# Moving one 256-token scale broadcast from behind a stage's last transposes to between its last two groups of transposes

## The chip, the cores and the metric

The kernel runs on one core of a Trainium2 chip. The metric is the device time of one execution in microseconds (us). PE is the matrix engine (TensorE; PEld is its weight loads), DVE the vector engine, ACT the scalar engine, POOL is GpSimd, SP issues most transfers.

## What is computed

One transformer-like block on 256 tokens of width 2048, then a final RMSNorm, all in float32. Cut to what the change touches:

```python
def rms_norm(x, w):
    y = xf * lax.rsqrt(jnp.mean(xf * xf, axis=-1, keepdims=True) + NORM_EPS)
    return y * w

def reference(...):
    n = rms_norm(h, norm_mix_w)
    h = h + token_mixer(n, ...)          # 8 delta heads, 8 x 3 windowed heads, then w_out
    n = rms_norm(h, norm_ffn_w)          # the second norm
    h = h + conv_gated_mlp(n, w_ffn_in, conv_ffn_w, w_ffn_out)   # 2048 -> 2 x 5632 -> 2048
    return rms_norm(h, norm_final_w)
```

The second norm has two factors: the weight `norm_ffn_w` by channel and the reciprocal root by token. The kernel applies the first when it transposes `h`, and the second, which commutes with the matrix product, only to the results of `w_ffn_in`.

## The kernel before, in words

**Weights.** All weight matrices stream through four raw buffers (`raws`, 1 MB each) by transfers that SP issues (`refill`, line 255). The products have float32 accuracy made of fast passes: each piece of weights is split into a high part `hi` (ACT, line 265) and a rest `lo` (DVE, line 266), each in four buffers, and activations are held as high and low halves too (`xcat[:, k, :256]` and `xcat[:, k, 256:]` for the 16 blocks k of 128 channels).

**Items.** The work of PE is a list of items. An item of `cm_block` (lines 303 to 322) covers one half of the 2048 input channels for 128 output channels: eight blocks k, three matmuls each (lines 314, 315, 316: `hi` with the high half of `xcat`, `hi` with its low half, `lo` with its high half), so 24 matmuls of 128x128 weights on 256 columns, into one PSUM bank. An item of `v_slab` (lines 382 to 384) has the tokens as weights, also 24 matmuls of 256 columns. Items of `tm_group` (lines 1224 to 1226, for `w_out` and `w_ffn_out`) use 512 columns. `run_items` splits the weights of three items ahead, writes one item's matmuls, then calls `pump`, which lets side work put its instructions behind that item. So the order on every engine is fixed when the program is written; nothing is scheduled later.

**Side work** consists of generators: each step up to a `yield` is one packet of instructions. `g_norm2(s, hb)` is one, for each quarter s of the 2048 channels of `h`: it squares and sums `h` by token (ACT, line 1275), then for each of two pairs of channel blocks takes a spare PSUM bank from `SB` (two banks), transposes four 128x128 tiles on PE (line 1282), writes the high half of `xcat` with the channel weight (ACT, line 1286) and the low half (DVE, line 1290). For s = 3, the last quarter, it then finishes the scale by token: sum and mean on DVE (lines 1295, 1296), the power -1/2 on POOL (line 1297), and two matmuls with the identity that spread the 256 scales over 128 partitions (line 1301), copied to `rbc` by ACT (line 1302). `rbc` (it lies in the tile `rC`) is first read by `up_hook` (line 1378), when the first output block of `w_ffn_in` is complete.

**The join of the two stages.** The stage of `w_ffn_in` has 22 x 8 = 176 items. Its first eight are reordered: first the four that read the channel blocks 0 to 7, then the four that read 8 to 15, so that matmuls can start before the last quarter of `h` is transposed. Five items of the stage run (`run_items(n_out + 5)`) while the side work of the second norm is still being written; `flush` then writes what is left of it. The 171 items that follow have no side work on PE at all.

Of the kernel before, what the change touches and what calls it, by code (L numbers as in the profile page):

```python
# [7 lines left out]
AF = mybir.ActivationFunctionType  # L8
ALU = mybir.AluOpType

P = 128
T = 256
D = 2048
# [5 lines left out]
EPS = 1e-6  # L19
# [66 lines left out]
def block_kernel(tc, A, out, dbg=None):  # L86
# [4 lines left out]
    ACT = nc.scalar.activation  # L91
    V = nc.vector
    G = nc.gpsimd
    mm = nc.tensor.matmul
# [15 lines left out]
    def pool(name, **kw):  # L110
        g = tc.tile_pool(name=name, bufs=1, reuse_waits="tile", **kw)
        return g, g.__enter__()
# [11 lines left out]
    SB = Slots(banks[6:8])  # L124

    cst = cp.tile([P, C_N], F32, name="cst")
    ident = cst[:, C_ID : C_ID + P]
    tri = [cst[:, C_TRI + o * P : C_TRI + (o + 1) * P] for o in range(2)]
    blk = cst[:, C_BLK : C_BLK + P]
    neghalf = cp.tile([P, 8], F32, name="neghalf")  # L130
# [10 lines left out]
    ss = cp.tile([P, 8, 2, H], F32, name="ss")  # L141
# [18 lines left out]
    done = set()  # L160
# [66 lines left out]
    def take(slots):  # L227
        while not slots.free:
            yield 0
        return slots.get()  # L230
# [221 lines left out]
    for k2 in range(8):  # L452
        bk = DB.get()
# [755 lines left out]
    go, op = None, None  # L1209
# [41 lines left out]
    go, op = pool("outp", side="left")  # L1251
# [3 lines left out]
    hss = cp.tile([P, 2, 4], F32, name="hss")  # L1255
    rbc = rC
# [5 lines left out]
    def o_hook(s):  # L1262
        hb = hs[s % 2]
        for t in range(2):
            V.tensor_add(hb[:, t, :], obanks[s][t], xr[s % 2][:, t, :])
        if s < 2:
            nc.gpsimd.dma_start(xr[s], xtok[:, :, (s + 2) * 512 : (s + 3) * 512])
        nc.gpsimd.dma_start(h_tok[:, :, s * 512 : (s + 1) * 512], hb)
        spawn(g_norm2(s, hb))
# [3 lines left out]
    def g_norm2(s, hb):  # L1273
        for t in range(2):
            ACT(sq, hb[:, t, :], AF.Square, accum_out=hss[:, t, s : s + 1])
        yield 0
        for k2 in range(2):
            bk = yield from take(SB)
            for e in range(2):
                kl = 2 * k2 + e  # L1280
                for t in range(2):
                    nc.tensor.transpose(bk[:, e * T + t * P : e * T + (t + 1) * P], hb[:, t, kl * P : (kl + 1) * P], ident)
            for e in range(2):
                k = 4 * s + 2 * k2 + e
                src = bk[:, e * T : (e + 1) * T]
                ACT(xcat[:, k, :T], src, AF.Copy, scale=nw_ffn[:, k : k + 1])
            for e in range(2):
                k = 4 * s + 2 * k2 + e
                src = bk[:, e * T : (e + 1) * T]
                stt(xcat[:, k, T:], src, nw_ffn[:, k : k + 1], xcat[:, k, :T].bitcast(F32), op0=ALU.mult, op1=ALU.subtract)  # L1290
            SB.put(bk)
            yield 700
        done.add(("n2", s))
        if s == 3:
            V.tensor_reduce(out=ss[:, 0, 0:2, 0:1], in_=hss, axis=mybir.AxisListType.X, op=ALU.add)
            V.tensor_scalar(ss[:, 1, 0:2, 0:1], ss[:, 0, 0:2, 0:1], 1.0 / D, EPS, op0=ALU.mult, op1=ALU.add)
            G.tensor_tensor(ss[:, 2, 0:2, 0], ss[:, 1, 0:2, 0], neghalf[:, 0:2], op=ALU.pow)
            yield 300
            bk = yield from take(SB)
            for t in range(2):  # L1300
                mm(bk[:, t * P : (t + 1) * P], lhsT=ss[:, 2, t, 0:1].to_broadcast([P, P]), rhs=ident, start=True, stop=True)
            ACT(rbc, bk[:, :T], AF.Copy)
            SB.put(bk)
            done.add("rbc")
            yield 0

# [179 lines left out]
```

## Time and profile before

| | us |
|---|---|
| three runs | 1543.66, 1540.58, 1543.41; median 1543.41 |
| the profiled execution | 1541.09, its span 1539.3 |
| PE busy in the span | 1513.6 (98%), 11531 matmuls |
| DVE, ACT, POOL busy | 1039.7 (68%), 828.2 (54%), 168.7 (11%) |
| PE busy from 792 to 1291 (the stage of `w_ffn_in`) | 499.00 of 499.00, granted clock 1.00 |
| PE busy from 1291 to 1539 (`w_ffn_out` and the end) | 239.75 of 248.00 |

A matmul's record lasts longer than the time to the next one's start, because matmuls overlap; the time from start to start is what PE spends on each. The granted clock is a share of 2.4 GHz. One matmul with float32 operands, as in line 1301, leaves two records in the trace, so the broadcast's two matmuls show as four; a transpose leaves one.

### The profile page before, as it was taken

What the parts mean: (1) busy time and instruction counts of PE and PEld (TensorE: products, weight loads), DVE (VectorE), ACT (ScalarE), POOL (GpSimd) and SP (SyncE); (2) the same over time, 40 slices, a digit from 0 to 9 for tenths busy, and PEclk for the clock granted to TensorE, in tenths of its full rate; (3) what the DMA queues carried; (4) which work ended last, traced back from release to release, by engine and by line L of the source; (5) the groups of instructions that cost most, each with busy time, mean ns of one, the idle gap of its engine ahead of it and who ended that gap; (6) DMA issues with size and microseconds to landing.
All of it is one profiled execution on the core that took longest, in us unless ns stands there. A gap on an engine that the chain in (4) does not pass through costs nothing.

```text
span 1539.3 us, 28194 instructions
## 1 busy us (share of the span) xinstructions
PE 1513.6 (98%) x11531; PEld 1442.5 (94%) x11531; DVE 1039.7 (68%) x1703; ACT 828.2 (54%) x1430; POOL 168.7 (11%) x257
## 2 busy tenths in 40 slices
PE   7999999999999999998999999999999999999997
PEld 7999999999999999997889999999999999888886
DVE  5878978879865666764557777677776766455454
ACT  5598875645556546653555545454454454344342
POOL 3254553000022202100000000000000000000000
PEclk9999999999999999998999999999999999999999
DMA  9657789746667636633765565565655557566552
GB/s 255 220 182 225 235 293 231 223 152 193 191 155 238 218 115 194 211 133 133 259 210 192 166 206 177 187 197 166 206 176 188 195 167 265 197 206 205 192 191 82
DMA packets 247699, 301.21 MB, mean 196 GB/s; under 512 B 11397, under 2 KB 208182, under 8 KB 247186
## 3 DMA queue, kind: packets, MB, share of 16 engines
q1 hardware_dynamic: 235602, 269.81, 54.8%
q0 software_dynamic: 11536, 29.02, 6.1%
q8 instruction: 90, 1.47, 0.4%
q10 hardware_dynamic: 432, 0.59, 0.1%
q14 instruction: 39, 0.32, 0.1%
HBM read 285.69 MB, written 13.65 MB: 194 GB/s over the span
## 4 chain that ended last, share of the span: by engine, by line
PE 95%; ACT 2%; issue 1%; DVE 1%; DMA 0%; POOL 0%; POOLq 0%; SPq 0%; ACTq 0%; DVEq 0%
PE bank L314 20%; PE bank L316 20%; PE bank L315 20%; PE bank L1224 7%; PE bank L1225 7%; PE bank L1226 7%; PE bank L382 3%; PE bank L383 3%; PE bank L384 3%; PE bank L978 1%; PE bank L1024 1%; PE bank L1019 1%; ACT hi L265 1%; PE bank L1198 1%; DMA xt<-in_x_dram 0%
## 5 line engine op out<-in xcount | busy, mean ns | idle before, releaser
L266 DVE TENSOR_TENSOR lo<-raw,hi 128x1024 fp32r<-128x1024 f32 x504 | 620.9, 1233 | 394.8 <-ACT hi L265 392.4
L265 ACT ACTIVATE hi<-raw 128x1024 fp32r<-128x1024 f32 x504 | 533.6, 1060 | 554.9 <-PE bank L315 252.1
L314 PE MATMUL bank<-xcat,hi 128*128 128x256 f32 x2688 | 757.5, 282 | 0.3 <-ACT pad L329 0.3
L315 PE MATMUL bank<-xcat,hi 128*128 128x256 f32 x2688 | 751.2, 279 | 0.0
L316 PE MATMUL bank<-xcat,lo 128*128 128x256 f32 x2688 | 751.0, 279 | 0.0
L315 PEld LDWEIGHTS bank<-xcat,hi 128*128 128x128 f32 x2688 | 511.2, 190 | 0.0
L314 PEld LDWEIGHTS bank<-xcat,hi 128*128 128x128 f32 x2688 | 505.7, 188 | 2.9 <-issue 0.9
L316 PEld LDWEIGHTS bank<-xcat,lo 128*128 128x128 f32 x2688 | 504.8, 188 | 0.0
L1225 PE MATMUL bank<-lo,gth 128*128 128x512 f32 x336 | 130.8, 389 | 0.0
L1226 PE MATMUL bank<-hi,gtl 128*128 128x512 f32 x336 | 130.8, 389 | 0.0
L1224 PE MATMUL bank<-hi,gth 128*128 128x512 f32 x336 | 130.8, 389 | 0.0
L382 PE MATMUL bank<-hi,xcat 128*128 128x256 f32 x384 | 109.2, 284 | 0.0
L384 PE MATMUL bank<-hi,xcat 128*128 128x256 f32 x384 | 107.0, 279 | 0.0
L383 PE MATMUL bank<-lo,xcat 128*128 128x256 f32 x384 | 107.0, 279 | 0.0
L1226 PEld LDWEIGHTS bank<-hi,gtl 128*128 128x128 f32 x336 | 63.1, 188 | 13.1
L1224 PEld LDWEIGHTS bank<-hi,gth 128*128 128x128 f32 x336 | 63.1, 188 | 13.1
L1225 PEld LDWEIGHTS bank<-lo,gth 128*128 128x128 f32 x336 | 63.1, 188 | 12.9
L382 PEld LDWEIGHTS bank<-hi,xcat 128*128 128x128 f32 x384 | 72.6, 189 | 0.5
L384 PEld LDWEIGHTS bank<-hi,xcat 128*128 128x128 f32 x384 | 72.4, 189 | 0.0
L383 PEld LDWEIGHTS bank<-lo,xcat 128*128 128x128 f32 x384 | 72.2, 188 | 0.0
L1391 DVE SCALAR_TENSOR_TENSOR fy<-fpad,cwf,fy 128x256 f32<-128x256 f32 x132 | 63.5, 481 | 2.4
L1421 POOL DMA_DIRECT2D nfb<-in_norm_final_w_dram x1 | 0.6, 585 | 485.7 <-PE bank L316 485.7
(299 smaller groups left out, 1447.9 us busy)
## 6 DMA issues: line engine op xcount, KB each, us to landing
raw<-in_w_in_dram SPq DMA_DIRECT2D x104, 1024.0 KB, 5.5
raw<-in_w_ffn_in_dram SPq DMA_DIRECT2D x88, 1024.0 KB, 5.1
raw<-in_w_ffn_out_dram SPq DMA_DIRECT2D x44, 1024.0 KB, 5.0
raw<-in_w_out_dram SPq DMA_DIRECT2D x14, 1024.0 KB, 5.1
rec_d<-rec POOLq DMA_DIRECT2D x8, 768.0 KB, 7.4
rr<-rec_d POOLq DMA_DIRECT2D x6, 512.0 KB, 4.6
xt<-in_x_dram SPq DMA_DIRECT2D x4, 512.0 KB, 8.4
gam<-cg_d POOLq DMA_DIRECT2D x8, 256.0 KB, 7.5
```

The lines of the kernel that those rows point to most:

```text
L265: ACT(hi, src, AF.Copy)
L266: V.tensor_sub(lo, src, hi.bitcast(F32))
L314: mm(acc, lhsT=hi[:, kk, :], rhs=xcat[:, k, :T], start=k == 0, stop=False)
L315: mm(acc, lhsT=hi[:, kk, :], rhs=xcat[:, k, T:], start=False, stop=False)
L316: mm(acc, lhsT=lo[:, kk, :], rhs=xcat[:, k, :T], start=False, stop=k == KT - 1)
L382: mm(o, lhsT=xh, rhs=hi[:, kk, :], start=k == 0 and t == 0, stop=False, skip_group_check=True)
L383: mm(o, lhsT=xh, rhs=lo[:, kk, :], start=False, stop=False, skip_group_check=True)
L384: mm(o, lhsT=xl, rhs=hi[:, kk, :], start=False, stop=k == KT - 1, skip_group_check=True)
L1224: mm(a[t], lhsT=xh, rhs=hi[:, kk, :], start=st, stop=False)
L1225: mm(a[t], lhsT=xh, rhs=lo[:, kk, :], start=False, stop=False)
L1226: mm(a[t], lhsT=xl, rhs=hi[:, kk, :], start=False, stop=sp_)
L1391: stt(y, pad[:, d : d + T], cwf[:, d, b : b + 1], y, op0=ALU.mult, op1=ALU.add)
```

## The change

For the last quarter (s = 3) the sum, mean and power move ahead of the first `yield`, in front of both groups of transposes, and the two broadcast matmuls with their copy move in front of the second group (`k2` = 1). Nothing is added or dropped.

```diff
     def g_norm2(s, hb):
         for t in range(2):
             ACT(sq, hb[:, t, :], AF.Square, accum_out=hss[:, t, s : s + 1])
+        if s == 3:
+            V.tensor_reduce(out=ss[:, 0, 0:2, 0:1], in_=hss, axis=mybir.AxisListType.X, op=ALU.add)
+            V.tensor_scalar(ss[:, 1, 0:2, 0:1], ss[:, 0, 0:2, 0:1], 1.0 / D, EPS, op0=ALU.mult, op1=ALU.add)
+            G.tensor_tensor(ss[:, 2, 0:2, 0], ss[:, 1, 0:2, 0], neghalf[:, 0:2], op=ALU.pow)
         yield 0
         for k2 in range(2):
+            if s == 3 and k2:
+
+                bk = yield from take(SB)
+                for t in range(2):
+                    mm(bk[:, t * P : (t + 1) * P], lhsT=ss[:, 2, t, 0:1].to_broadcast([P, P]), rhs=ident, start=True, stop=True)
+                ACT(rbc, bk[:, :T], AF.Copy)
+                SB.put(bk)
+                done.add("rbc")
+                yield 0
             bk = yield from take(SB)
...
         done.add(("n2", s))
-        if s == 3:
-            V.tensor_reduce(out=ss[:, 0, 0:2, 0:1], in_=hss, axis=mybir.AxisListType.X, op=ALU.add)
-            V.tensor_scalar(ss[:, 1, 0:2, 0:1], ss[:, 0, 0:2, 0:1], 1.0 / D, EPS, op0=ALU.mult, op1=ALU.add)
-            G.tensor_tensor(ss[:, 2, 0:2, 0], ss[:, 1, 0:2, 0], neghalf[:, 0:2], op=ALU.pow)
-            yield 300
-            bk = yield from take(SB)
-            for t in range(2):
-                mm(bk[:, t * P : (t + 1) * P], lhsT=ss[:, 2, t, 0:1].to_broadcast([P, P]), rhs=ident, start=True, stop=True)
-            ACT(rbc, bk[:, :T], AF.Copy)
-            SB.put(bk)
-            done.add("rbc")
-            yield 0
```

How the order of instructions moves. The changed file has its own line numbers: there the broadcast is line 1286, its copy 1287, the transposes 1295, the high halves 1299, the low halves 1303, the sum and mean 1277 and 1278. Each "..." below stands for the rest of an item's 24 matmuls.

PE at the join of the stages, before (`hs` holds `h`, `cst` the identity, `ss` the scales; the items' banks are 71 to 74):

```order
L1282 MATMUL bank_77<-cst,hs_8008 128x128 x4
L314 MATMUL bank_71<-xcat,hi_100 128x256
...
L1282 MATMUL bank_78<-cst,hs_8008 128x128 x4
L314 MATMUL bank_72<-xcat,hi_101 128x256
...
L314 MATMUL bank_73<-xcat,hi_98 128x256
...
L1301 MATMUL bank_77<-cst,ss 128x128 x2
L314 MATMUL bank_74<-xcat,hi_99 128x256
```

The broadcast is the last thing that stands between items; behind it come 171 items in one row.

PE at the same place, with the change:

```order
L1295 MATMUL bank_77<-cst,hs_8008 128x128 x4
L314 MATMUL bank_71<-xcat,hi_100 128x256
...
L1286 MATMUL bank_78<-cst,ss 128x128 x2
L314 MATMUL bank_72<-xcat,hi_101 128x256
...
L1295 MATMUL bank_77<-cst,hs_8008 128x128 x4
L314 MATMUL bank_73<-xcat,hi_98 128x256
...
L314 MATMUL bank_74<-xcat,hi_99 128x256
```

There are still three groups between the same items, one item apart now, but the last one consists of four transposes and stands directly in front of the first item that reads the channel blocks 8 to 15. From that item on 172 items follow in one row.

ACT at the same place, before:

```order
L1286 ACTIVATE xcat<-bank_77,nw_ffn 128x256 x2
L265 ACTIVATE hi_99<-raw_94 128x1024
L1286 ACTIVATE xcat<-bank_78,nw_ffn 128x256 x2
L265 ACTIVATE hi_100<-raw_95 128x1024
L265 ACTIVATE hi_101<-raw_95 128x1024
L1302 ACTIVATE rC<-bank_77 128x256
```

and with the change:

```order
L1299 ACTIVATE xcat<-bank_77,nw_ffn 128x256 x2
L265 ACTIVATE hi_99<-raw_94 128x1024
L1287 ACTIVATE rC<-bank_78 128x256
L265 ACTIVATE hi_100<-raw_95 128x1024
L1299 ACTIVATE xcat<-bank_77,nw_ffn 128x256 x2
L265 ACTIVATE hi_101<-raw_95 128x1024
```

The copy to `rC` has taken the place of the last pair of high halves, and that pair stands one split later. DVE moves in the same way (sum and mean in front of the first `lo`, the last pair of low halves one `lo` later); the queues of SP and POOL keep their order.

## Rows read from the trace of the kernel before

**Rows 1.** The page's part 4: the chain that ended last, by engine.

```profile
PE 95%; ACT 2%; issue 1%; DVE 1%; DMA 0%; POOL 0%; POOLq 0%; SPq 0%; ACTq 0%; DVEq 0%
```

**Rows 2.** Windows: stretch, length, busy us (xrecords) PE PEld DVE ACT POOL, PEclk, DMA share, GB/s.

```profile
219.00:283.00 64.00, 64.00 (x568) 64.00 (x567) 52.15 (x91) 36.23 (x58) 22.39 (x38) 1.00 1.01 251
337.00:391.00 54.00, 54.00 (x479) 54.00 (x478) 48.59 (x65) 30.55 (x47) 0.00 (x0) 1.00 0.64 202
284.00:298.00 14.00, 14.00 (x120) 14.00 (x119) 13.66 (x20) 8.57 (x15) 0.00 (x0) 1.00 0.73 227
810.00:1290.00 480.00, 480.00 (x4077) 480.00 (x4077) 340.91 (x514) 242.51 (x344) 0.00 (x0) 1.00 0.57 186
```

**Rows 3.** Timeline of PE at the join: start us, us, engine, line, operation.

```profile
801.48 0.60 PE L1282 MATMUL bank<-cst,hs 128*128 128x128 f32 x4
801.83 0.37 PE L314 MATMUL bank<-xcat,hi 128*128 128x256 f32 x1
...
804.67 0.28 PE L314 MATMUL bank<-xcat,hi 128*128 128x256 f32 x1
...
807.05 0.28 PE L314 MATMUL bank<-xcat,hi 128*128 128x256 f32 x1
...
807.39 0.60 PE L1301 MATMUL bank<-cst,ss 128*128 128x128 f32 x4
...
808.19 0.28 PE L314 MATMUL bank<-xcat,hi 128*128 128x256 f32 x1
...
810.66 0.28 PE L314 MATMUL bank<-xcat,hi 128*128 128x256 f32 x1
```

**Rows 4.** Timeline of PE where items of line 314 give way to line 382.

```profile
283.56 0.28 PE L316 MATMUL bank<-xcat,lo 128*128 128x256 f32 x1
283.68 0.28 PE L382 MATMUL bank<-hi,xcat 128*128 128x256 f32 x1
```

**Rows 5.** Timeline of PE: transposes between items, two, two, eight and four of them.

```profile
65.41 0.38 PE L692 MATMUL bank<-cst,rec 128*128 128x128 f32 x2
...
185.33 0.38 PE L692 MATMUL bank<-cst,vt 128*128 128x128 f32 x2
...
310.48 1.04 PE L1179 MATMUL bank<-cst,sm 128*128 128x128 f32 x8
...
311.71 0.28 PE L382 MATMUL bank<-hi,xcat 128*128 128x256 f32 x1
...
313.95 0.28 PE L383 MATMUL bank<-lo,xcat 128*128 128x256 f32 x1
...
528.62 0.28 PE L382 MATMUL bank<-hi,xcat 128*128 128x256 f32 x1
...
530.98 0.28 PE L384 MATMUL bank<-hi,xcat 128*128 128x256 f32 x1
531.10 0.60 PE L900 MATMUL bank<-cst,oo 128*128 128x128 f32 x4
...
531.89 0.28 PE L382 MATMUL bank<-hi,xcat 128*128 128x256 f32 x1
...
533.82 0.28 PE L384 MATMUL bank<-hi,xcat 128*128 128x256 f32 x1
```

**Rows 6.** Timeline of ACT, DVE and POOL at the join of the stages.

```profile
797.28 0.19 ACT L1275 ACTIVATION_READ_ACCUMULATOR sq<-hs 128x1 f32 x1
...
802.12 0.84 ACT L1286 ACTIVATE xcat<-bank,nw_ffn 128x256 fp32r<-128x256 f32 x2 [1.39 <-PE bank L1282]
802.84 1.06 ACT L265 ACTIVATE hi<-raw 128x1024 fp32r<-128x1024 f32 x1
802.99 0.88 DVE L1290 SCALAR_TENSOR_TENSOR xcat<-bank,nw_ffn,xcat 128x256 fp32r<-128x256 f32 x2 [1.00 <-ACT xcat L1286]
...
805.08 0.15 DVE L1295 TENSOR_REDUCE ss<-hss 128x2 f32<-128x8 f32 x1
...
805.53 0.71 POOL L1297 TENSOR_TENSOR ss<-ss,neghalf 128x2 f32<-128x2 f32 x1 [7.96 <-DVE ss L1296]
...
808.03 0.38 ACT L1302 ACTIVATE rC<-bank 128x256 f32<-128x256 f32 x1 [2.21 <-PE bank L1301]
```

**Rows 7.** The page's part 6: transfers, KB each, median us from issue to landing.

```profile
h_d<-hs POOLq DMA_DIRECT2D x4, 512.0 KB, 5.5
```

## The prediction

> **What bounds the kernel now.** I read three views in this order. The chain that ended last says that PE makes up 95% of it [rows 1]: what doesn't change PE's time changes nothing. The windows then show that PE has no idle time at all from 810 to 1290, at a granted clock of 1.00 [rows 2]. So in this stage the bound isn't a wait; it is the time from the start of one matmul to the next. The third view is the timeline of PE, read for exactly that, and there is the surprise: **the same matmul has two paces.** A window counts every matmul that it touches, so the pace is (length + 0.28) / count. From 219 to 283 and from 337 to 391 it is 64.28/568 and 54.28/479 us, 113.2 and 113.3 ns. From 810 to 1290 it is 480.28/4077 us, 117.8 ns. Lines, tile shape and clock are the same [rows 2]. More work on the other engines isn't the cause: DVE was busier in the fast stretches (52.15 of 64 and 48.59 of 54 us against 340.91 of 480), and in the first of them the transfers' share was 1.01 against 0.57.
>
> Where does the pace change? At the join of the two stages, to the matmul. Over 21 matmuls ahead of the broadcast the pace is (807.05 - 804.67)/21 = 113 ns; over 21 behind it, (810.66 - 808.19)/21 = 118 ns [rows 3]. Behind it nothing stands between the matmuls until the stage ends at 1291, and the pace stays slow to the end. So I followed every stretch of 256-column matmuls through the timeline and noted its pace and what stood in front of it. The result is a pattern that I can't explain, but that holds well:
>
> - A pace is **kept** while items of one kind follow each other. I counted 93 steps from a fast item directly to another of its kind; all 93 stayed fast. Of 190 steps from a slow item, 188 stayed slow; the other two had a pause of PE in them.
> - It is lost where items of line 314 give way to line 382, or the reverse: four times in four, as at 283.68 [rows 4], behind which the window has 14.28/120 us, 119 ns [rows 2]. The coming stage has no such place.
> - It is **set anew** by whatever stands between items. One, two or four transposes alone: 25 cases, the first at 65.41 [rows 5], the last at 801.48 [rows 3]; 24 leave the fast pace, one, at 185.33, the slow one [rows 5]. Of these the six cases of four transposes are all fast, and so are all six cases that came from a slow stretch; the one at 531.10 is both: (530.98 - 528.62)/20 = 118 ns ahead of it, (533.82 - 531.89)/17 = 114 ns behind [rows 5]. Eight transposes: 4 of 4 slow, as at 310.48, (313.95 - 311.71)/19 = 118 ns behind it [rows 5]. Groups of four or eight plain matmuls: mostly slow, the broadcast among them.
>
> **The change, part by part.**
>
> *PE.* The same three groups stand between items, so no instruction comes or goes: the broadcast's gap is 0.60 of overlapped records as the transposes' is [rows 3], and moving it costs nothing by itself. What moves is which group is last. It was the broadcast (slow behind it); it will be four transposes (fast behind them in 6 cases of 6). The broadcast now stands one item earlier; taking its slow pace with it, that one item costs 24 x 4.5 ns = 0.1 us more. The stage has 176 items, 5 of them ahead of the old broadcast, so 171 x 24 = 4104 matmuls are at stake. At 117.8 - 113.3 = 4.5 ns each that is 18.5 us; less 0.1 it is **18.4 us**. The bounds of this term are 0 (transposes leave the slow pace, as at 185.33) and 18.4 us, and I take the upper one, since 24 of 25 cases lie there. The stage of 512-column items behind 1291 isn't counted: it follows the same matmuls either way.
>
> *The later pair of `xcat`.* This is the one new danger. The last transposes now stand directly in front of an item that reads their result; before, an item lay between. By the trace, transposes that start at 801.48 give ACT its pair of high halves 0.64 us later, and DVE its pair of low halves from 1.51 to 2.39 us after their start [rows 3, 6]. The item itself starts 0.35 us after them, and it uses the two new blocks as its seventh and eighth. Its eighth block starts 807.05 - 804.67 = 2.38 us into an item [rows 3], so the seventh at about 2.04, and the low half is the second matmul of a block, 0.11 later. The low halves are needed at about 0.35 + 2.15 = 2.50 and 0.35 + 2.49 = 2.84 us after the transposes' start, and are there at about 1.95 (half of the pair) and 2.39. Some 0.45 us are left. On ACT the split in front of the pair takes 1.06 us [rows 6]; it can start when the copy to `rC` ends, some 2 us before the pair is due, so it is out of the way. If it did stand in the way in full, PE would wait 1.06 - 0.45 = 0.6 us. Bounds 0 and 0.6 us; I take 0, by the row of the pair.
>
> *The broadcast's input.* It now needs the power before the second group. The sums are there at 797.28 + 0.19 = 797.47; from the start of the sum on DVE to the end of the power on POOL took 805.53 + 0.71 - 805.08 = 1.16 us [rows 6]. So the scales are ready at about 798.6, and PE comes to the broadcast at about 801.5: 2.9 us to spare. On POOL only the transfer issue of `h_d` stands ahead of it, as before.
>
> *ACT, DVE, SP.* The copy to `rC` (0.38 us) moves from 808.03 to about 802.1 [rows 6], long before its first reader. The split behind the last pair comes about 1.3 us later than before, for an item that PE reaches three items later; the refill that waits for its DVE half is as much later, with three other buffers full. Cost 0: the cover is that lead of three items, 8 us.
>
> **Sum.** Against the profiled execution: 1541.1 - 18.4 = 1522.7 us. The median of the runs shown is 2.3 us above that execution (1543.4), and a new measurement is more like the median: 1543.4 - 18.4 = **1525.0 us**, a share of 0.988.
>
> The Trainium skill has a rule against this. Its page "TensorE: Matmul & The Clock Gate", section "Back-to-back issue gap", gives a warm matmul a fixed time from start to start, columns / 2.4 GHz + 2.5 ns, an estimate of 109 ns for 256 columns, whatever came before. By it the order of groups would be worth nothing, and the sum would be 0. The trace doesn't agree: neither pace is 109, and there are two.
>
> **The rivals.**
>
> *Nothing happens:* the last transposes leave the slow pace, or the pace hangs on something else than the groups. For it: one case in 25, and that no transposes stood exactly here before. Against it: the same four transposes, in front of items of the same line with the same buffers, left 113 ns behind them twice, the last at 801.48 [rows 3]. Time: 1543.4, with the 0.6 us wait 1544. The rule of the Trainium skill's page above would give this time too.
>
> *Fast, but not to the end.* A stage of 171 items is longer than the longest fast stretch that I saw (24 items). If the pace falls back after n items, the gain is n x 24 x 4.5 ns, 0.108 us per item: with n = 86 the time is 1534. Against it: 93 steps of 93.
>
> *Another engine becomes the bound.* The stage would need 186 x 117.8/113.3 = 193 GB/s and DVE 74% of the time. The fast stretches ran at 251 and 202 GB/s with DVE at 81% and 90% [rows 2], without a pause on PE. I give it no chance of its own.
>
> *Slower:* the broadcast waits for POOL, now in the middle of the matmuls. It decides when the power ends later than 801.5. The nearest row that could make it late is the transfer of `h_d` that POOL issues in front of it: if POOL were held until that lands, 5.5 us after its issue at about 796.9 [rows 7], the power would end at 803.1 and PE would lose 1.6 us; with a second such hold-up, 7.1 us. If the last transposes also left the slow pace, that is 1545 to 1550.5. Against it: before, issue and power had nothing between them but idle time (7.96 us [rows 6]).
>
> **How the numbers follow.** About 0.2%, 3.1 us, is what a measurement of this kernel can tell from no change. Fast to the end: 24 of 25 for the transposes, 93 of 93 for keeping it over a stage longer than any seen; together I say 0.78. Fast in part: 0.04. Nothing: 0.15. Slower: 0.03. So faster 0.82, same 0.15, slower 0.03. The likeliest case has its own range: from the fastest run shown, 1540.6 - 18.4 = 1522.2, less 0.4 us for a tenth of a ns in the paces, to 1525.0 plus 0.6 for the wait and as much as the runs scatter, 1527. To hold 8 in 10 the upper end goes to 1533, which takes in about half of the cases that are fast in part.
>
> **What would show it.** Right: behind the last transposes a pace of 113 ns that lasts, 450 us of the stage with some 3970 matmuls (450.28/0.1133) in place of 3820, the switch to 512 columns some 18 us earlier, no wait of PE for `xcat` or for the power. Wrong: 117.8 ns behind the transposes (my reading of what sets the pace fails); 113 ns at first and 118 later (it isn't kept); a wait of PE in the item behind the transposes (the timing of the pair was too tight).

## The result, and the profile after

The changed kernel took 1522.4 us (median of four executions, 1521.21 to 1523.29), the kernel before 1542.5 us (median of four, 1540.58 to 1543.66). The ratio is 0.9875, with a 95% interval from 0.9863 to 0.9887: 1.25% faster, which is 19.3 us (the two medians by themselves lie 20.1 us apart, the two profiled spans 19.9). The forecast was 1525.0 us in a range from 1521.8 (its 1522.2 - 0.4) to 1533.

First the busy times. The page's part 1 of the changed kernel, whose span is 1519.4 us:

```profile
PE 1494.4 (98%) x11531; PEld 1423.3 (94%) x11531; DVE 1037.6 (68%) x1703; ACT 828.4 (55%) x1430; POOL 170.3 (11%) x257
```

The number of instructions is the same, PE's share is the same, and its busy time is 19.2 us less than the 1513.6 us before. So PE did the same matmuls in less time each; no wait went away. The chain that ended last has PE at 95%, as in [rows 1].

Next the windows, which count how many matmuls fit into the same length. Columns as in [rows 2]. The kernel before:

```profile
690.00:715.00 25.00, 20.03 (x91) 16.44 (x90) 11.57 (x33) 8.68 (x21) 2.81 (x4) 0.80 0.19 60
810.00:1260.00 450.00, 450.00 (x3823) 450.00 (x3823) 319.57 (x482) 226.88 (x321) 0.00 (x0) 1.00 0.57 185
```

The changed kernel:

```profile
690.00:715.00 25.00, 20.04 (x98) 16.54 (x97) 12.97 (x34) 8.85 (x24) 2.81 (x4) 0.93 0.23 74
810.00:1260.00 450.00, 450.00 (x3973) 450.00 (x3972) 330.79 (x500) 235.52 (x334) 0.00 (x0) 1.00 0.59 193
```

In the 450 us inside the stage of `w_ffn_in`, PE is busy without a gap in both, at a granted clock of 1.00 in both, and it starts 3973 matmuls in place of 3823. The pace is 450.28/3973 = 113.3 ns against 450.28/3823 = 117.8 ns: the two paces of [rows 2]. The rows from 690 to 715 hold another, smaller difference, to which I come below.

Then the timeline. PE of the kernel before (start, length, engine, line, operation), at places that the changed kernel has too:

```profile
708.17 1.34 PE L900 MATMUL bank<-cst,oo 128*128 128x128 f32 x4 [3.17 <-DVE oo L895]
...
798.30 0.60 PE L1282 MATMUL bank<-cst,hs 128*128 128x128 f32 x4
...
1291.20 0.39 PE L1224 MATMUL bank<-hi,gth 128*128 128x512 f32 x1
```

PE of the changed kernel:

```profile
707.28 1.34 PE L900 MATMUL bank<-cst,oo 128*128 128x128 f32 x4 [3.16 <-DVE oo L895]
...
796.60 0.60 PE L1295 MATMUL bank<-cst,hs 128*128 128x128 f32 x4
...
799.77 0.60 PE L1286 MATMUL bank<-cst,ss 128*128 128x128 f32 x4
...
800.57 0.28 PE L314 MATMUL bank<-xcat,hi 128*128 128x256 f32 x1
...
802.92 0.28 PE L316 MATMUL bank<-xcat,lo 128*128 128x256 f32 x1
803.04 0.60 PE L1295 MATMUL bank<-cst,hs 128*128 128x128 f32 x4
803.40 0.37 PE L314 MATMUL bank<-xcat,hi 128*128 128x256 f32 x1
...
805.65 0.28 PE L315 MATMUL bank<-xcat,hi 128*128 128x256 f32 x1
...
805.99 0.28 PE L315 MATMUL bank<-xcat,hi 128*128 128x256 f32 x1
...
806.22 0.28 PE L314 MATMUL bank<-xcat,hi 128*128 128x256 f32 x1
...
810.98 0.28 PE L314 MATMUL bank<-xcat,hi 128*128 128x256 f32 x1
...
1271.34 0.39 PE L1224 MATMUL bank<-hi,gth 128*128 128x512 f32 x1
```

Three things are to be read here.

- **The slow pace went with the broadcast.** In the one item behind it, (802.92 - 800.57)/20 = 117.5 ns; behind the last four transposes, (810.98 - 806.22)/42 = 113.3 ns. In [rows 3] it is the other way round in time: 113 ahead of the broadcast, 118 behind it.
- **The stage gained 18.16 us.** From the first of the three groups to the first 512-column matmul it took 1291.20 - 798.30 = 492.90 us before and 1271.34 - 796.60 = 474.74 us after.
- **The other 1.7 us were there ahead of the join**, where both kernels run the same instructions. At the transposes of line 900 the changed kernel is 0.89 us ahead, at the join 1.70. Around that place the windows from 690 to 715 show a mean granted clock of 0.80 and 0.93: some 10 us and 3.5 us at half the clock, in a stretch in which PE waits several times for DVE (3.17 and 3.16 us in the lines above). Nothing of the change reaches that place, so I don't count it as its effect. The traces of the runs below bear this out: two of them (the broadcast as two transposes, and two transposes in the middle of the row) are at half the clock there for about 10 us as well, the other five edits at the join for 3.4 or 6.8 us, whether they came out fast or slow.

Last, the engines around it. ACT, DVE and POOL of the changed kernel at the join:

```profile
796.24 0.71 POOL L1279 TENSOR_TENSOR ss<-ss,neghalf 128x2 f32<-128x2 f32 x1 [0.38 <-DVE ss L1278]
...
800.41 0.39 ACT L1287 ACTIVATE rC<-bank 128x256 f32<-128x256 f32 x1 [1.39 <-PE bank L1286]
...
803.68 0.84 ACT L1299 ACTIVATE xcat<-bank,nw_ffn 128x256 fp32r<-128x256 f32 x2 [1.94 <-PE bank L1295]
...
804.55 0.87 DVE L1303 SCALAR_TENSOR_TENSOR xcat<-bank,nw_ffn,xcat 128x256 fp32r<-128x256 f32 x2 [1.55 <-ACT xcat L1299]
```

The power ends at 796.95, 2.8 us ahead of the broadcast. The late pair of `xcat` is complete at 805.42, and PE reads its low halves at 805.65 and 805.99 without a gap.

### The profile page after: what moved, and what is told of

It is laid out like the page before. It is cut to its first block, busy times and chain, and to the rows that moved or that the text cites. A ratio compares the mean times of both kernels' runs of the same rounds, so it can differ in the third digit from the quotient of the medians.

```text
span 1519.4 us, 28192 instructions
## 1 busy us (share of the span) xinstructions
PE 1494.4 (98%) x11531; PEld 1423.3 (94%) x11531; DVE 1037.6 (68%) x1703; ACT 828.4 (55%) x1430; POOL 170.3 (11%) x257
## 4 chain that ended last, share of the span: by engine, by line
PE 95%; ACT 2%; issue 1%; DVE 1%; DMA 0%; POOL 0%; POOLq 0%; SPq 0%; ACTq 0%; DVEq 0%
PE bank L314 20%; PE bank L316 19%; PE bank L315 19%; PE bank L1224 7%; PE bank L1225 7%; PE bank L1226 7%; PE bank L382 3%; PE bank L383 3%; PE bank L384 3%; PE bank L978 1%; PE bank L1024 1%; PE bank L1019 1%; ACT hi L265 1%; ACT gam L591 1%; DMA xt<-in_x_dram 0%
```

## The experiments

The result shows that the stage runs at another pace, and that the change of pace sits at its last group. It doesn't show which property of that group does it. The expectations name theories by letters. **A** is the prediction's: the kind of the last group sets the pace of the row behind it, transposes fast, plain matmuls slow. **B** puts it down to the scale by token coming earlier. **C** says that the pace is fixed for the whole stage at the join. **D** says that the moment at which the row starts again decides, so the length of the group and the pace in front of it. **E** is a clash of addresses, and **G** a pause in front of the group. All groups that are added are unused work: their results go to a spare PSUM bank that nobody reads.

The four runs that came first undo or add one part each, beside the kernel before at 1540.3 us.

**Four more transposes behind the old broadcast** (edit of the kernel before):

```diff
+            junk2 = yield from take(SB)
             for t in range(2):
                 mm(bk[:, t * P : (t + 1) * P], lhsT=ss[:, 2, t, 0:1].to_broadcast([P, P]), rhs=ident, start=True, stop=True)
+            for i in range(4):
+                nc.tensor.transpose(junk2[:, i * P : (i + 1) * P], ident, ident)
...
+            SB.put(junk2)
```

> The kernel before, with four idle transposes of the identity written directly behind the broadcast into the other spare bank, so that four transposes are the last group ahead of the 171 items. Theory A (the kind of the last group ahead of the row of items sets its pace): 113.3 ns behind them, 1542.5 - 18.3 + 0.5 for the added transposes = about 1524.7 us. Theory B (what helps is that the scale by token and its copy come earlier): nothing is earlier here, 117.8 ns and about 1543 us.

Measured: 1523.5 us, ratio 0.9891 [0.9874, 0.9909]. The broadcast stays where it was, and nearly all of the gain is there.

**The broadcast as two transposes** (edit of the kernel before, same place, same values):

```diff
-                mm(bk[:, t * P : (t + 1) * P], lhsT=ss[:, 2, t, 0:1].to_broadcast([P, P]), rhs=ident, start=True, stop=True)
+                nc.tensor.transpose(bk[:, t * P : (t + 1) * P], ss[:, 2, t, 0:1].to_broadcast([P, P]), ident)
```

> The kernel before, the broadcast at its old place but done by two transposes of the spread scale in place of two matmuls with the identity; the result is the same. Theory A: two transposes left the fast pace in 18 of 19 cases, so 113.3 ns and about 1524 us. Theory B: nothing is earlier, about 1542.5 us.

Measured: 1523.6 us, ratio 0.9887 [0.9871, 0.9902]. Nothing was moved at all, and the gain is the same as the change's within the intervals.

**A second, unused broadcast behind the last transposes** (edit of the changed kernel):

```diff
+        if s == 3:
+            bk = yield from take(SB)
+            for t in range(2):
+                mm(bk[:, t * P : (t + 1) * P], lhsT=ss[:, 2, t, 0:1].to_broadcast([P, P]), rhs=ident, start=True, stop=True)
+            SB.put(bk)
+            yield 0
```

> The changed kernel with a second, unused broadcast (two matmuls, no copy) one item behind the last transposes. Theory A: the plain group is last again, 117.8 ns from there on, 1522.4 + 18.3 + 0.4 = about 1541 us. Theory B: the scale is as early as in the changed kernel, 1522.8 us.

Measured: 1541.2 us, ratio 1.0007 [0.9997, 1.0016]. Two unused matmuls, one item behind the last transposes, take back everything.

**Only sum, mean and power early** (edit of the kernel before):

```diff
+        if s == 3:
+            V.tensor_reduce(...)
+            V.tensor_scalar(...)
+            G.tensor_tensor(...)
         yield 0
...
-            V.tensor_reduce(...)
-            V.tensor_scalar(...)
-            G.tensor_tensor(...)
-            yield 300
```

> The kernel before with only sum, mean and power moved ahead of the transposes; the broadcast stays last. Theory A: the last group is the same plain one, 117.8 ns, no change, 1542.5 us. Theory B: the scale's chain is as early as in the changed kernel, so most of the gain, about 1524 us.

Measured: 1541.1 us, ratio 1.0005 [0.9995, 1.0015]. The early scale by itself is worth nothing. (With the `yield 300` gone the broadcast also stands one item earlier here, and 172 items follow it, all slow.)

**Two transposes in the middle of the long row** (edit of the kernel before; behind 85 of the 171 items):

```diff
+    groups = {44: 'T2'}
+
+    def group(name):
...
+                nc.tensor.transpose(o, ident, ident)
...
     def up_hook(which, f, acc):
         pad = grab(fpad)
+        if 2 * f + which in groups:
+            group(groups[2 * f + which])
```

> The kernel before with one idle group of two transposes at the middle of the stage of w_ffn_in (in front of the 86 last of its 176 items); the broadcast stays where it was. Theory A (the last group sets the pace and it is kept): 117.8 ns up to the group and 113.3 behind it, a gain of 86 x 24 x 4.5 ns = 9.3 us less 0.14 for the group, about 1531 us against 1540.3 for the kernel before in the last comparison. Theory C (the pace is fixed for the whole stage at its start, by what stands at the join): no change.

Measured: 1532.5 us, ratio 0.9946 [0.9929, 0.9962], beside 1540.3. A pace can be set anew in the middle of the row, and half of the row gives half of the gain: 2064 matmuls x 4.5 ns = 9.3 us were to be had, and the ratio is worth 8.3 us (5.9 to 10.9).

The windows show it directly. Each fence has the stretch from 810 to 1030, and the one for the transposes in the middle also 1060 to 1260, behind them. Four transposes behind:

```profile
810.00:1030.00 220.00, 220.00 (x1943) 220.00 (x1942) 161.56 (x246) 116.48 (x165) 0.00 (x0) 1.00 0.60 194
```

The broadcast as transposes:

```profile
810.00:1030.00 220.00, 220.00 (x1944) 220.00 (x1943) 161.40 (x244) 116.47 (x165) 0.00 (x0) 1.00 0.60 194
```

Two transposes midway:

```profile
810.00:1030.00 220.00, 220.00 (x1871) 220.00 (x1870) 155.31 (x233) 112.29 (x159) 0.00 (x0) 1.00 0.58 187
1060.00:1260.00 200.00, 200.00 (x1767) 200.00 (x1766) 146.82 (x221) 103.60 (x148) 0.00 (x0) 1.00 0.60 196
```

1943 or 1944 matmuls in 220.28 us are 113.3 ns, 1871 are 117.7 ns, and 1767 in 200.28 us are 113.3 ns. There is nothing in between.

So far everything spoke for A. A table of small groups was to show whether it holds for other sizes: **72 unused groups between the items of the long row** (edit of the changed kernel; T1 to T8 are one to eight transposes of the identity, M1 to M4 one to four plain matmuls of it, in an order drawn by chance):

```diff
     def up_hook(which, f, acc):
         pad = grab(fpad)
+        if 2 * f + which in groups:
+            group(groups[2 * f + which])
```

> The changed kernel with 72 idle groups in the stage of w_ffn_in, one behind every second item: one to eight transposes of the identity, or one to four float32 matmuls of the identity with itself, six of each in a shuffled order. It is run for the pace behind each group, not for its time. Theory A as it stood in the prediction: up to four transposes leave 113.3 ns nearly always, eight 117.8, plain matmuls 117.8 mostly, whatever the pace was in front. Theory D (it isn't the kind but the phase in which the row starts again, so each group's length and the pace in front decide): the same group leaves different paces after a fast and after a slow stretch, in a way that repeats for all six of its cases.

Measured, as the share of groups with 113 ns behind them: M1 6/6, M2 6/6, M3 6/6, M4 6/6; T1 4/6, T2 1/6, T3 6/6, T4 1/6, T5 6/6, T6 6/6, T7 6/6, T8 5/6. (1563.95 us, with the time of the groups themselves.) **This is nearly A upside down**: plain groups of the identity are followed by the fast pace every time, two and four transposes nearly always by the slow one. The pace in front, which D counts as well, has to be kept in mind: 20 of the 24 plain groups stood behind a fast stretch.

That left D: not the kind, but the length of the group and the pace in front of it. Two runs put A and D against each other at the join, beside the kernel before at 1540.6 us. **The old broadcast lengthened by two unused plain matmuls** (edit of the kernel before), by D fast, since four plain matmuls of the identity were:

```diff
             done.add("rbc")
             yield 0
+            bk = yield from take(SB)
+            for i in range(2):
+                mm(bk[:, i * P : (i + 1) * P], lhsT=ident, rhs=ident, start=True, stop=True)
+            SB.put(bk)
+            yield 0
```

> The kernel before, its broadcast followed at once by two more idle matmuls of the identity with itself, so that the last group is still plain but four matmuls long in place of two. Theory A (the kind decides: plain groups leave the slow pace): 117.8 ns, 1540.3 + 0.45 = about 1540.8 us. Theory D (the exact moment at which the row of items starts again decides, so the group's length counts, not its kind): the table of groups had four plain matmuls of the identity fast in 6 cases of 6, so 113.3 ns and about 1522.5 us.

Measured: 1541.2 us, ratio 1.0004 [0.9994, 1.0014]: slow. D's forecast missed and A's, 1540.8 us, held. (Two of the four matmuls here are the broadcast's, so this isn't quite the group of the table.)

**Two transposes of the identity one item behind the last transposes** (edit of the changed kernel), by A fast, by D slow:

```diff
+        if s == 3:
+            bk = yield from take(SB)
+            for i in range(2):
+                nc.tensor.transpose(bk[:, i * P : (i + 1) * P], ident, ident)
+            SB.put(bk)
+            yield 0
```

> The changed kernel with one idle group of two transposes of the identity, one item behind its last transposes. Theory A: two transposes are a kind that leaves the fast pace, 113.3 ns, about 1522.6 us. Theory D: the table of groups had two transposes of the identity leave the slow pace in 4 of 5 cases behind a fast stretch, so 117.8 ns and about 1522.4 + 18.2 = 1540.7 us.

Measured: 1541.3 us, ratio 1.0004 [0.9994, 1.0014]: slow. A's forecast missed, and D's, 1540.7 us, held. PE's timeline of this run:

```profile
804.77 0.60 PE L1295 MATMUL bank<-cst,hs 128*128 128x128 f32 x4
805.12 0.37 PE L314 MATMUL bank<-xcat,hi 128*128 128x256 f32 x1
805.33 0.28 PE L315 MATMUL bank<-xcat,hi 128*128 128x256 f32 x1
...
805.56 0.28 PE L314 MATMUL bank<-xcat,hi 128*128 128x256 f32 x1
...
807.83 0.28 PE L316 MATMUL bank<-xcat,lo 128*128 128x256 f32 x1
807.95 0.38 PE L1310 MATMUL bank<-cst 128*128 128x128 f32 x2
808.09 0.36 PE L314 MATMUL bank<-xcat,hi 128*128 128x256 f32 x1
808.29 0.28 PE L315 MATMUL bank<-xcat,hi 128*128 128x256 f32 x1
...
808.52 0.28 PE L314 MATMUL bank<-xcat,hi 128*128 128x256 f32 x1
...
810.88 0.28 PE L316 MATMUL bank<-xcat,lo 128*128 128x256 f32 x1
```

Behind the four transposes of the kernel the pace is (807.83 - 805.56)/20 = 113.5 ns; behind the two unused ones it is (810.88 - 808.52)/20 = 118.0 ns. It was two unused transposes of the same identity that had brought the fast pace in the middle of the row. So kind and number don't decide by themselves. What differs between the two is the pace in front: slow in the middle of the row, fast here.

**Does the operand decide?** Again 72 groups, T and M as above, R1 to R8 transposes of the tile with the spread scales, N1 one plain matmul with it (edit of the changed kernel, same place as in the first table).

> The changed kernel with 72 idle groups in the stage of w_ffn_in, run for the pace behind each: one, two, three, four or eight transposes, of the identity (T) or of the tile with the scale (R), and one plain matmul of either (M, N); six of each in a shuffled order. Theory D: each kind behind a fast stretch repeats what it did in the first table (T2 and T4 mostly slow, T3 and T8 fast, M1 fast, T1 keeps the pace), and a group of the same length with other operands may differ, by its own timing, but repeats itself. Theory A (kind alone): T and R of the same length leave the same pace. If both fall, the same group leaves now one pace and now the other.

Measured: T1 5/6, T2 1/6, T3 5/6, T4 2/6, T8 4/6; R1 4/6, R2 0/6, R3 5/6, R4 1/6, R8 4/6; M1 2/6, N1 3/6. (1558.3 us.) Between transposes of the two tiles there is no clear difference. One and three transposes again were mostly followed by 113 ns, two and four by 118; but M1 fell from 6/6 to 2/6 in another order of the groups.

**Both tables and the kernel before, read by the pace in front of the group.** The fall of M1 has a reason. Over both tables M1 was followed by the fast pace in 8 of 8 cases behind a fast stretch and in 0 of 4 behind a slow one; N1 in 3 of 3 and 0 of 3, T1 in 8 of 8 and 1 of 4. So a single matmul or transpose mostly kept the pace that was there. Behind a fast stretch T3 was followed by the fast pace in 9 of 9 cases, T2 in 1 of 8 and T4 in 1 of 7. D's reading holds that far; for eight transposes it doesn't (T8 behind a fast stretch: 6 of 9).

The kernel's own pairs of plain matmuls say it most clearly. Line 994 has two of them, as the broadcast has, at a place ahead of the join that all kernels share. In the kernel before:

```profile
483.93 0.28 PE L314 MATMUL bank<-xcat,hi 128*128 128x256 f32 x1
...
486.28 0.28 PE L316 MATMUL bank<-xcat,lo 128*128 128x256 f32 x1
486.40 0.61 PE L994 MATMUL bank<-R,UB 128*128 128x128 f32 x4
...
487.21 0.28 PE L314 MATMUL bank<-xcat,hi 128*128 128x256 f32 x1
...
489.48 0.28 PE L316 MATMUL bank<-xcat,lo 128*128 128x256 f32 x1
```

The same instructions in the run with the broadcast as two transposes:

```profile
485.80 0.28 PE L314 MATMUL bank<-xcat,hi 128*128 128x256 f32 x1
...
488.07 0.28 PE L316 MATMUL bank<-xcat,lo 128*128 128x256 f32 x1
488.18 0.60 PE L994 MATMUL bank<-R,UB 128*128 128x128 f32 x4
...
488.99 0.28 PE L314 MATMUL bank<-xcat,hi 128*128 128x256 f32 x1
...
491.34 0.28 PE L316 MATMUL bank<-xcat,lo 128*128 128x256 f32 x1
```

In the first the pace is 2.35/20 = 117.5 ns in front of the pair and 2.27/20 = 113.5 ns behind it; in the second, where the item in front happened to be fast, it is 113.5 ns in front and 117.5 ns behind. Counted by the nanosecond starts of twelve traces (both kernels and the ten runs up to the pauses, but not the two further down that move the weights in their buffers), a pair of plain matmuls alone between items of lines 314 to 316 (lines 994 and 1019 and the broadcast, not the identity with itself) was followed by the other pace than the one in front of it in 130 cases of 130: 49 from fast to slow, 81 from slow to fast. Most of these are the same few places seen in twelve traces; in the kernel before alone it is 4 and 7. The broadcast is one of the 4. By this count it left the slow pace because the pace in front of it was fast, and not because it is plain; no run put it behind a slow stretch. The unused pairs of the identity with itself (M2) don't behave like that: the fast pace followed in 4 cases of 4 behind a fast stretch and in 2 of 2 behind a slow one.

**Does a pause decide?** 72 groups of one to four transposes of the tile that DVE has just written, so that PE has to wait before each (edit of the changed kernel):

```diff
         V.tensor_mul(pad[:, 1 : T + 1], acc[:, :T], rbc)
+        if 2 * f + which in groups:
+            for i in range(int(groups[2 * f + which][1:])):
+                nc.tensor.transpose(banks[6][:, i * P : (i + 1) * P], pad[:, 1 : P + 1], ident)
```

> The changed kernel with 72 idle groups of one to four transposes in the stage of w_ffn_in, each of the tile that DVE has just written, so that PE has to wait in front of the group. Run for the pace behind each group. Theory D (the moment of the restart decides): the wait makes that moment arbitrary, so each length leaves both paces, about as often as the first two tables together did (a little over half fast). Theory G (a pause of PE leads to the fast pace, as the two pauses inside slow stretches of the kernel before did): at least 9 in 10 of the groups that waited are followed by 113.3 ns.

Measured: 57 of 72 were followed by 113 ns, 15 by 118. That is fewer than G wants and more than D gives; it separates nothing, except that G's nine in ten isn't there. What it does show stands in the last section.

**Does the place of the weights decide?** `AT_CM` is the offset, in elements, at which the split weights of these items lie in their buffers. One run of the changed kernel and one of the kernel before with another offset:

```diff
-AT_CM, AT_OUT = 32, 72
+AT_CM, AT_OUT = 0, 72
```

> The changed kernel, with the high and low halves of the weights of this stage at the start of their buffers in place of 32 elements into them. Theory D: addresses don't matter, same groups, same moments, 113.3 ns and about 1522 us. Theory E (the slow pace is a clash of the addresses that PE reads): the paces themselves change, or the pace behind the last transposes does.

> The kernel before, with the same shift of the weights' halves to the start of their buffers. Theory D: 117.8 ns behind the broadcast and about 1540.5 us. Theory E: another slow pace than 117.8 ns, or the fast one.

Measured, one execution each, beside 1541.5 us: 1553.8 us with the change, 1550.8 us without it. With this offset the change brings nothing, and both are slower than any other kernel of the study except those with 72 groups. Windows of the changed kernel with offset 0:

```profile
337.00:391.00 54.00, 54.00 (x459) 53.89 (x458) 46.59 (x63) 28.14 (x44) 0.00 (x0) 1.00 0.52 158
830.00:1280.00 450.00, 450.00 (x3823) 450.00 (x3822) 319.95 (x482) 227.44 (x324) 0.00 (x0) 1.00 0.58 188
```

Of the kernel before with offset 0:

```profile
219.00:283.00 64.00, 64.00 (x546) 64.00 (x545) 51.65 (x89) 36.45 (x62) 26.50 (x43) 1.00 1.00 245
```

The stretches that were fast in [rows 2], with 568 and 479 matmuls, now hold 546 and 459: 117.7 and 118.3 ns. In the stage of `w_ffn_in` the same four transposes at the same place leave 450.28/3823 = 117.8 ns behind them. Ahead of the join, of 3817 steps from one matmul of lines 314 to 316 to the next, 2902 took under 115.5 ns in the kernel before and 2772 in the changed one; with offset 0 it is 415 and 236. The two paces themselves are the same as ever. What moves is how often a restart takes the fast one: with offset 0 all 22 pairs of plain matmuls that stood behind a slow stretch of these items left it slow, where with offset 32 all 81 left the fast pace.

## Why the prediction was right, and which of its reasons was not

- **The bound.** PE's time from start to start, not a wait: right. Instructions, waits and clock in the stage are the same, and the time went by the pace.
- **The term of the sum.** 4104 matmuls x 4.5 ns - 0.1 = 18.4 us were forecast, 18.16 us measured from the join to the 512-column items. (The broadcast went from behind the fifth item to behind the third, not by one item as the prediction has it; that one item runs at the slow pace for it is right all the same.) The 3973 matmuls in 450 us stand against "some 3970", the transfer rate of 193 GB/s against 193, and DVE's 330.79/450 = 74% against 74%.
- **Kept to the end.** Right: 172 items in a row stayed fast, where 24 had been the longest stretch seen. The half gain from the middle of the row says the same of both paces.
- **The later pair of `xcat`.** Low halves were forecast from 1.51 to 2.39 us after the transposes and came from 804.55 - 803.04 = 1.51 to 2.38; PE read them at 2.61 and 2.95, forecast 2.50 and 2.84. No wait.
- **The power on POOL.** Forecast 2.9 us to spare, measured 2.8. The copy to `rC` came at 800.41, as early as forecast once the 1.70 us are taken off.
- **The remainder.** 1525.0 - 1522.4 = 2.6 us. Some 0.9 us is the baseline, whose median with a fourth execution is 1542.5 in place of 1543.4. Another 1.7 us were won ahead of the join, around the stretch at half clock near 707 us, which is shorter in the profile of the changed kernel. It can't be called a gain of the change: its length varies from run to run, and the changed kernel's four executions fall into two near 1521.4 and two near 1523.2, and its profile was one of the faster.
- **What sets the pace: right here, wrong as a rule.** The prediction wrote that a pace "is set anew by whatever stands between items" and took "24 of 25 cases" of transposes as the chance of this one. That it is set at such a place held in every run. That the kind of the group sets it did not. It left out the pace in front of the group: two plain matmuls such as the broadcast reverse it, in 4 and 7 cases of the kernel before's own trace, so "mostly slow" was a mean over two different conditions. And 20 of the 25 cases of transposes are groups of one line, 692. At the join A holds for the kernel's own groups (with transposes last the changed kernel and two edits of the kernel before are fast; with a broadcast last the kernel before and two edits are slow), but two transposes of the identity one item later are slow, plain groups of the identity elsewhere are fast, four transposes of it were followed by the fast pace in only 3 of 12 cases of the tables, and with another offset of the weights the same transposes are slow. For the kernel's own four transposes there was direct evidence, two cases of two at the join itself (at 798.30 and 801.48); that the rule of kinds pointed the same way was in part luck, and a pattern that can't be explained deserved less than the 0.78 it was given.
- **A rule against it.** The Trainium skill's page "TensorE: Matmul & The Clock Gate", section "Back-to-back issue gap", gives the gap of an isolated warm matmul as columns / 2.4 GHz + 2.5 ns, with no term for what stood ahead of it; the prediction made a rival of that, at 1543.4 us. The same section says that this formula leaves out the weight load, and that in a stream of weight loads and matmuls both set the spacing, so it spoke less clearly against the change than the prediction says. The measurement disagrees with one figure for all rows by 1.25%: at the same granted clock of 1.00 the same instruction took 113.3 or 117.8 ns.

**What stays open** is what decides the pace at a restart. Shown is that it is decided there, that it is kept, and that the pace in front of the group and the offset of the weights take part. Neither kind, number, operand nor length of the group is enough, also together with the pace in front: two transposes behind a fast stretch were followed by the fast pace in 14 of 15 cases at line 692 of the kernel before, and in 1 of 8 in the tables. Nor does every place decide the same way each time: of 70 rows ahead of the join with at least 20 matmuls of lines 314 to 316, which all kernels share, 61 had the same pace in all twelve traces with the kernel's own offset, and nine did not. None of the twelve runs gives a rule that holds for all the groups tried here. No version beat the changed kernel; the two that equal it are the broadcast written as transposes and the four unused transposes behind it. An edit that the pairs of plain matmuls suggest, the broadcast behind a slow stretch, was not tried at the head of the long row.

## What to carry to other kernels

Where PE is 100% busy, count matmuls of one form in stretches of equal length: if the same instruction has two paces at the same clock, the last thing ahead of a long row may be worth more than any wait. Try several small edits at that place (another order, another form of the same operation, another offset of the buffers) and measure each, since here no rule could tell beforehand which one wins. Sort the cases also by the pace in front of the place: a pair of matmuls that looked "mostly slow" turned out to reverse the pace. And treat a count such as 24 of 25 as evidence for the place where it was counted, not as a law about the kind of instruction.

## What the runs showed of the hardware that was not expected

- **Two paces that last.** A row of some 4100 matmuls keeps the pace of its first few. It can be told early: in the nanosecond starts of the twelve traces with the kernel's own offset, among rows of at least 20 matmuls of lines 314 to 316, a first step (first to second matmul of the row) of 205 to 208 ns was followed by the fast pace in 303 cases of 303; with 200 to 204 ns it was 229 fast and 263 slow. In the timeline of the two unused transposes it shows as 805.33 - 805.12 = 0.21, fast, and 808.29 - 808.09 = 0.20, slow. This is a sign, not a cause: with offset 0 five rows began with 205 ns, and all five were slow.
- **A pair of plain matmuls reverses the pace.** At the kernel's own offset, between items of lines 314 to 316, in 130 cases of 130; pairs of the identity with itself don't (6 of 6 fast behind them). Why, no run shows.
- **An offset of 32 elements in a buffer is worth some 9 us.** 1550.8 against 1541.5 us in the kernel before, one execution of each, with no instruction more or less.
- **A pause of 2.7 us costs more than itself.** In the run with pauses, PE's timeline around one of them:

```profile
965.21 0.28 PE L316 MATMUL bank<-xcat,lo 128*128 128x256 f32 x1
968.17 0.96 PE L1384 MATMUL bank<-cst,fpad 128*128 128x128 f32 x4 [2.68 <-DVE fpad L1381]
...
969.14 0.41 PE L315 MATMUL bank<-xcat,hi 128*128 128x256 f32 x1
969.36 0.41 PE L316 MATMUL bank<-xcat,lo 128*128 128x256 f32 x1
...
971.86 0.28 PE L316 MATMUL bank<-xcat,lo 128*128 128x256 f32 x1
...
975.75 0.28 PE L316 MATMUL bank<-xcat,lo 128*128 128x256 f32 x1
```

and the windows behind it:

```profile
969.00:971.50 2.50, 2.50 (x14) 2.50 (x14) 0.36 (x1) 0.00 (x0) 0.00 (x0) 0.50 0.00 0
972.00:975.00 3.00, 3.00 (x28) 3.00 (x27) 0.73 (x1) 1.06 (x1) 0.00 (x0) 1.00 0.00 0
```

PE started its last matmul at 965.21, then waited 2.68 us for DVE, and from 968.17 on ran at a granted clock of 0.50 (1.2 GHz), 0.21 us from start to start, until about 971.7; behind that the clock is 1.00 again, and the pace in this case (975.75 - 971.86)/33 = 117.9 ns. Each of the 72 pauses was followed by such a stretch. The run took 1867.8 us: the 72 pauses with what follows them cost (1867.8 - 1522.4)/72 = 4.8 us each, groups included.
